# A gated attention block on one core: load order of the first tokens, shorter rotary angles, and the query latent between transposes

## The chip, the cores and the metric

The kernel runs on one core of a Trainium2 chip. The metric is the device time of one execution, in microseconds (us); the median of the runs before the change is 751.84. A core has five engines that run side by side: TensorE (PE in the profile; its weight loads are PEld), VectorE (DVE), ScalarE (ACT), GpSimd (POOL) and SyncE (SP), which here issues the transfers. A transfer is carried by 16 DMA engines, whichever engine issued it.

## The reference

One decoder layer on 512 tokens of width 1024, all in float32:

```
xn   = RMSNorm(x)
proj = xn @ w_in          # split into q_lat 384 | kv_lat 256 | k_rope 32 | dq, dk, dv 512 each | gates 2048
branch A: q = RMSNorm(q_lat) @ w_uq ; k, v = RMSNorm(kv_lat) @ w_ukv ; rotary on 32 dims ; causal attention, 8 heads
branch B: rotary on 16 of 64 dims ; (softmax(q1 k1) - lambda softmax(q2 k2)) v ; RMSNorm per head, 4 heads
merged = sigmoid(gate_a) * (o_a @ w_a) + sigmoid(gate_b) * (o_b @ w_b)
x = x + merged @ w_out
x = x + (silu(hn @ w_gate) * (hn @ w_up)) @ w_down,  hn = RMSNorm(x)
out = RMSNorm(x)
```

The rotary angles are position x inverse frequency; their sine and cosine are taken after the angle is reduced to a part of one turn.

## The kernel before, in words

**Products.** A float32 product is made from three products of a rounded type: each operand is split into `hi` (rounded) and `lo` (the residue, `src - hi`), and `mm3` (L299 to L303) adds hi x hi, hi x lo and lo x hi. Every weight and every activation that TensorE multiplies therefore needs two element-wise operations first: a rounding (a copy with a type change) and a residue (a subtraction). Which engine does which is set by lists: `W_DVE` names the latent weights whose rounding is on VectorE (the others are on ScalarE), `W_POOL` those whose residue is on GpSimd (the others on VectorE), and `W_ENG0`, `W_ENG`, `W_ENG_DIFF` do the same for the weights that `weights` loads later, in three stages.

**Tiles.** Tokens are in four tiles of 128 (`NB = 4`), the model width in eight chunks of 128 (`KD = 8`). `xts[t]` is token tile t as loaded, in two halves of 512 columns. `scaled_transpose(t0, t1)` transposes these tiles on TensorE (L347), scales with the norm's gain while it rounds out of PSUM (ACT, L353), and writes the residue (DVE, L355); the result is `xn`. The factor 1/rms is applied later, so that the products need not wait for it; `x_square` (L359) gathers the sums of squares.

**The first 50 us.** `LOADS` is the order of the first transfers, all issued by SP: `r` the gains and biases as rows (`rows`), `x0` to `x3` the token tiles, `A0` to `A6` two chunks each of the query-latent weights, `B0` to `B6` the same for the key-value latent, `i` the frequency column and the positions. `START` is the order of the work on them: `r` makes columns from `rows` by a transpose after eight dummy products (`columns`, L216), `t0`, `t1`, `t23` transpose token tiles, `d6` runs six dummy products, `a0`...`b7` split latent weights (`latent_weights`, L325), `s0`...`s3` are the sums of squares. Then come, in the order of the program, the norm factors, lambda (L387 to L393), the rotary angles (L398 to L417), their sines on ScalarE with a change of activation table before and after (L420 to L435), and the latents.

`latent(b)` (L443) multiplies token tiles by the latent weights: b = 0 the query latent (128 x 384, `PS("mm")`, and `"pv"` for the last tile), b = 1 key-value latent and rotary key (128 x 288). For each tile there are 8 chunks of 3 products; ACT then squares with a sum (L449) and copies (L451). After the first two tiles of b = 1 the rotary tables are multiplied out on TensorE (L540), then the rest follows, and then the fill work: gate products, projections and attention.

**Order.** A scheduler that simulates the engines orders each engine's instructions, by priority in the order of the program among what it takes to be ready. `tc.issue_after(x)` adds an order: instructions of the block on x's engine come behind x. Each engine works its instructions off in that order, so one that waits holds up all behind it. Slots of the pools (`L` 22, `w` 3, `raw` 4) come free when their users are done.

**The angles.** With `ahl` an angle in two parts, and a sum over five pieces of 1/(2 pi), a piece costs a multiply-and-round (L405, L406), a plain multiply (L407), a subtraction (L409 or L411) and, after the first, an addition (L412), all on VectorE on 128 x 256.

Of the kernel before, what the change touches and what calls it, by code (L numbers as in the profile page):

```python
# [16 lines left out]
AF = mybir.ActivationFunctionType  # L17
ALU = mybir.AluOpType
# [13 lines left out]
QR, KVR, RD = 384, 256, 32  # L32
# [4 lines left out]
MAGIC = 12582912.0  # L37
TWO_PI = 6.283185
BUFS = dict(X=2, L=22, P=6, PT=1, raw=4, w=3, t=5, sm=24)
LOADS = "r x0 A0 i A2 x1 A4 A6 x2 x3 B0 B2 B4 B6".split()  # L40
START = "r t0 d6 a0 a1 a2 a3 t1 s0 s1 a4 a5 a6 a7 t23 s2 s3 b0 b1 b2 b3 b4 b5 b6 b7".split()
TAB_T = 2
LAST = 256
W_POOL = "a0 a1 a4 b0 b1 b2 b3 b4 b5 b6 b7".split()
W_DVE = "b0 b1 b2 b3 b4 b5 b6 b7".split()
N_WARM = 8
P_POOL = (0, 1)
W_ENG0 = ['act', 'pool']
# [45 lines left out]
def build(ctx, nc, tc, a, out):  # L94
# [12 lines left out]
    def PS(tag):  # L107
        return pp.tile([P, 512], F32, name=nm("ps_" + tag), tag=tag, bufs=PBUFS[tag])
# [4 lines left out]
    def LF():  # L113
        return T("L", [P, 1024], F32)
# [4 lines left out]
    def sm(w=1):  # L119
        return T("sm", [P, w], F32)  # L120

    def r32(ap):
        return ap.bitcast(F32)

    def dma(o, i):
        nc.sync.dma_start(out=o, in_=i)
# [18 lines left out]


    LOG_EXP = "natural_log_exp_and_others"
    table = [nc.scalar.preload_act_table_set(LOG_EXP)]

    def load_log_exp(after):  # L150
        with tc.issue_after(after.ins):
# [18 lines left out]
    ones = sb.tile([P, P], F32, name="ones")  # L170
    nc.vector.memset(ones, 1.0)

    def load_x(t):
        for c in range(2):
            dma(xts[t][:, c * S:(c + 1) * S], a["x"][0, t * P:(t + 1) * P, c * S:(c + 1) * S])

    misc = T("PT", [P, 2560], F32)

    def latent_load(b, k):
        c0, n = ((0, QR), (C_KV, KVR + RD))[b]  # L180
        if b == 1 and k == 6:
            v = misc[:, 11 * P:11 * P + 2 * n]
        else:
            i = k % 4 if b == 0 else k
            v = r32(lat_raw[k // 4 if b == 0 else 2]).rearrange("p a b -> p (a b)")[:, i * n:(i + 2) * n]
        v = v.rearrange("p (a b) -> p a b", a=2)
        dma(v, kview("w_in", c0, n, k, 2))
        for j in range(2):
            lat_w[k + j][b] = v[:, j, :]

    lat_w = [[None, None] for _ in range(KD)]
    ccol = sb.tile([P, 2], F32, name="ccol")
    cst, lv = misc[:, 0:4 * P], misc[:, 4 * P:6 * P].rearrange("p (i d) -> p i d", i=4)
# [10 lines left out]
        dma(pos_i, a["positions"])  # L204

    for step in LOADS:
        k = int(step[1:] or 0)
        if step[0] == "x":
            load_x(k)
        elif step[0] == "r":  # L210
            dma(rows, a["rows"])
        elif step[0] == "i":
            small_inputs()
        else:
            latent_load("AB".index(step[0]), k)
    def columns():  # L216
        dummies(N_WARM)
        pc = PS("sc")
        nc.tensor.transpose(out=pc[:, :30], in_=rows, identity=ident[:30, :30])
        nc.vector.tensor_copy(out=cols, in_=pc[:, :30])  # L220
        nc.vector.tensor_scalar(out=cols[:, R_SG:R_SG + 1], in0=cols[:, R_SG:R_SG + 1], scalar1=1.0 - LAMBDA_INIT,
                                scalar2=None, op0=ALU.mult)
# [35 lines left out]
                                           op0=ALU.mult, op1=ALU.subtract)  # L258

    w_eng = list(W_ENG0)  # L260

    def round_hi(o, i):
        if w_eng[0] == 'act':
            nc.scalar.activation(out=o, in_=i, func=AF.Copy)  # L264
        else:
            nc.vector.tensor_copy(out=o, in_=i)

# [31 lines left out]
    def mm3(o, lhs, rhs, start, stop):  # L299
        (lh, ll), (rh, rl) = lhs, rhs  # L300
        nc.tensor.matmul(out=o, lhsT=lh, rhs=rh, start=start, stop=False)  # L301
        nc.tensor.matmul(out=o, lhsT=lh, rhs=rl, start=False, stop=False)  # L302
        return nc.tensor.matmul(out=o, lhsT=ll, rhs=rh, start=False, stop=stop)  # L303
# [16 lines left out]
        return [T("X", [P, 4, 2, S], F32R) for _ in range(2)]  # L320


    last_t, last_hi = [None], [None]

    def latent_weights(b, k):  # L325
        raw = lat_w[k][b]
        n = (QR, KVR + RD)[b]
        w = T("L", [P, 2, n], F32R)
        if "ab"[b] + str(k) in W_DVE:
            nc.vector.tensor_copy(out=w[:, 0, :], in_=raw)  # L330
        else:
            nc.scalar.activation(out=w[:, 0, :], in_=raw, func=AF.Copy)
        (nc.gpsimd if "ab"[b] + str(k) in W_POOL else nc.vector).tensor_sub(out=w[:, 1, :], in0=raw, in1=r32(w[:, 0, :]))
        lat_w[k][b] = [w[:, s, :] for s in range(2)]

# [3 lines left out]
    def scaled_transpose(t0, t1):  # L339

        n = t1 - t0
        for k0 in range(0, KD, 4 // n):
            pt = PS("tr" if k0 // (4 // n) % 2 == 0 else "sc")
            c = 0
            for k in range(k0, k0 + 4 // n):
                for t in range(t0, t1):
                    last_t[0] = nc.tensor.transpose(out=pt[:, c:c + P], in_=xts[t][:, k * P:(k + 1) * P], identity=ident)  # L347
                    c += P
            parts = [[pt[:, (k - k0) * n * P:(k - k0 + 1) * n * P]]
                     + [xn[k // 4][:, k % 4, s_, t0 * P:t1 * P] for s_ in range(2)] + [col(R_XG + k)]  # L350
                     for k in range(k0, k0 + 4 // n)]
            for src, hi, lo, g in parts:
                last_hi[0] = nc.scalar.activation(out=hi, in_=src, func=AF.Identity, scale=g)  # L353
            for src, hi, lo, g in parts:
                nc.vector.scalar_tensor_tensor(out=lo, in0=src, scalar=g, in1=r32(hi), op0=ALU.mult, op1=ALU.subtract)  # L355

    def x_square(t):
        with tc.issue_after(last_hi[0].ins):
            nc.scalar.activation(out=xts[t], in_=xts[t], func=AF.Square, accum_out=x_ss[:, t:t + 1])  # L359

    for step in START:
        k = int(step[1:2] or 0)
        if step[0] == "r":
            columns()
        elif step[0] == "d":
            with tc.issue_after(last_t[0].ins):
                dummies(int(step[1:]))
        elif step[0] in "ab":
            latent_weights("ab".index(step[0]), k)
        else:  # L370
            if step[0] == "s":
                x_square(k)
            else:
                scaled_transpose(k, int(step[-1]) + 1)

    dma(cst, a["cst"][:, 0:4 * P])
    dma(misc[:, 4 * P:6 * P], a["lambdas"].broadcast_to([P, 256]))

    def xa(k, sl=slice(None)):
        return [xn[k // 4][:, k % 4, s, sl] for s in range(2)]  # L380

    x_rs = rsqrt(x_ss, D, NB)
    x_ms = sm(NB)
    nc.vector.tensor_mul(out=x_ms, in0=x_rs, in1=x_rs)

    lp = lv[:, 0:4:2, :]
    nc.vector.tensor_mul(out=lp, in0=lv[:, 0:4:2, :], in1=lv[:, 1:4:2, :])  # L387
# [13 lines left out]
    ahl, acc, ry, rx = [v[:, c:c + 2 * P].rearrange("p (s n) -> p s n", s=2) for v in (tmp(), tmp()) for c in (0, 2 * P)]  # L401
    nc.vector.tensor_copy(out=ahl[:, 0, :], in_=r32(ah))
    nc.vector.tensor_sub(out=ahl[:, 1, :], in0=ang, in1=ahl[:, 0, :])
    for j, c in enumerate(_inv_2pi_pieces()):
        nc.vector.tensor_scalar(out=ry, in0=ahl, scalar1=c, scalar2=MAGIC, op0=ALU.mult, op1=ALU.add)  # L405
        nc.vector.tensor_scalar(out=ry, in0=ry, scalar1=MAGIC, scalar2=0.0, op0=ALU.subtract, op1=ALU.add)  # L406
        nc.vector.tensor_scalar(out=rx, in0=ahl, scalar1=c, scalar2=0.0, op0=ALU.mult, op1=ALU.add)  # L407
        if j == 0:
            nc.vector.tensor_sub(out=acc, in0=rx, in1=ry)  # L409
        else:  # L410
            nc.vector.tensor_sub(out=rx, in0=rx, in1=ry)  # L411
# [12 lines left out]
    for src in (turn_c, turn):  # L424
        tg = tmp()
        nc.gpsimd.memset(tg, 0.0)
        for q in range(4):
            with tc.issue_after(last_sin.ins):
                last_sin = nc.scalar.activation(out=tg[32 * q:32 * q + 32, q * P:(q + 1) * P],
                                                in_=src[32 * q:32 * q + 32, :], func=AF.Sin, scale=TWO_PI)  # L430
# [6 lines left out]
    latn = [LF() for _ in range(NB)]

    lat_ss = [sm(NB), sm(NB)]

    lat_mm = [None]

    def latent(b, t0=0, t1=NB):  # L443
        c0, n, ncol = ((0, QR, QR), (QR, KVR + RD, KVR))[b]
        for t in range(t0, t1):
            ps = PS("pv" if t == 3 and b == 0 else "mm")
            for k in range(KD):
                lat_mm[0] = mm3(ps[:, :n], xa(k, slice(t * P, (t + 1) * P)), lat_w[k][b], k == 0, k == KD - 1)
            nc.scalar.activation(out=latn[t][:, c0:c0 + ncol], in_=ps[:, :ncol], func=AF.Square,  # L449
                                 accum_out=lat_ss[b][:, t:t + 1])  # L450
            nc.scalar.activation(out=latn[t][:, c0:c0 + n], in_=ps[:, :n], func=AF.Copy)  # L451

    def latent_norm(b):
        c0, ncol = ((0, QR), (QR, KVR))[b]
# [68 lines left out]
    ps = PS("sc")  # L523
# [283 lines left out]
    for p in range(4):  # L807
        o = L_()
# [56 lines left out]
    x1 = []  # L865
# [135 lines left out]
```

## Time and profile before

| what | value |
|---|---|
| median of 3 runs | 751.84 us (751.84 to 752.97) |
| the profiled execution: time, span | 753.9 us, 752.1 us |
| mean granted TensorE clock | 0.993 |
| busy: PE, DVE, ACT, POOL | 737.0, 414.7, 326.8, 104.3 us |
| moved by DMA | 76.74 MB, mean 102 GB/s |

The span runs from the first to the last instruction; the profiled execution took 1.8 us more than its span, and 2.1 us more than the median. In the timeline a line has start, duration, engine, line of the kernel, operation, output and inputs, shape, count, and in brackets the idle time before it with what ended it. In the busy time by stages a line has the stretch, its length, busy time and count for PE, PEld, DVE, ACT and POOL, the granted clock, the share of the DMA engines and GB/s. In the waits a line has who waited for whom: total, times, longest.

### The profile page before, as it was taken

The numbers are of one execution on the slowest core, as the hardware profiler recorded it, in microseconds if no ns is written. First come the engines' busy times: TensorE is split into PE (matmuls) and PEld (weight loads), VectorE is DVE, ScalarE is ACT, GpSimd is POOL, SyncE is SP. The second block draws the span as 40 slices with busy tenths as digits, with TensorE's granted clock in tenths as the row PEclk, the third lists the DMA queues.
The fourth block names the chain that finished last, engine by engine and source line by source line (L and its number), as shares of the span: only waits on it lengthen the run. The fifth ranks groups of instructions, "written<-read, shape, count | busy, mean of one in ns | idle before, by whom it ended". The sixth has DMA issues, their size and how long they took to land.

```text
span 752.1 us, 9652 instructions
## 1 busy us (share of the span) xinstructions
PE 737.0 (98%) x3639; PEld 623.0 (83%) x3639; DVE 414.7 (55%) x800; ACT 326.8 (43%) x609; POOL 104.3 (14%) x94
## 2 busy tenths in 40 slices
PE   7999999999999999999999999999999999999996
PEld 5988889888888888788898888888888888888885
DVE  6968688898998745595453323333333332122424
ACT  6564558587667535644233323232322223122314
POOL 3505252631341001000000000000000000000302
PEclk9999999999999999999999999999999999999999
DMA  8404333552433322248023333333323232322203
GB/s 300 124 1 117 106 87 96 135 126 69 110 87 87 107 85 85 84 140 278 2 85 108 89 97 99 98 99 87 109 85 111 85 112 85 109 88 92 106 0 113
DMA packets 99820, 76.74 MB, mean 102 GB/s; under 512 B 6303, under 2 KB 86973, under 8 KB 99773
## 3 DMA queue, kind: packets, MB, share of 16 engines
q1 hardware_dynamic: 99773, 76.12, 34.3%
q8 instruction: 29, 0.48, 0.3%
q14 instruction: 18, 0.15, 0.1%
HBM read 69.81 MB, written 2.10 MB: 96 GB/s over the span
## 4 chain that ended last, share of the span: by engine, by line
PE 81%; DVE 9%; ACT 5%; POOL 2%; issue 2%; DMA 1%; SPq 0%; DVEq 0%; ACTq 0%
PE ps_mm L301 22%; PE ps_mm L303 22%; PE ps_mm L302 22%; PE ps_sc L633 2%; PE ps_sc L301 1%; PE ps_sc L302 1%; PE ps_tr L301 1%; PE ps_tr L302 1%; PE ps_tr L303 1%; PE ps_sc L303 1%; POOL t L567 1%; PE ps_tr L659 1%; ACT L L495 1%; DVE w L269 1%; DVE X L355 1%
## 5 line engine op out<-in xcount | busy, mean ns | idle before, releaser
L302 PE MATMUL ps_mm<-X,w 128*128 128x512 f32 (+1 forms) x568 | 217.0, 382 | 0.0
L301 PE MATMUL ps_mm<-X,w 128*128 128x512 f32 (+1 forms) x568 | 216.9, 382 | 0.1
L303 PE MATMUL ps_mm<-X,w 128*128 128x512 f32 (+1 forms) x568 | 216.6, 382 | 0.0
L269 DVE TENSOR_TENSOR w<-raw,w 128x1024 fp32r<-128x1024 f32 x92 | 116.3, 1266 | 165.4 <-ACT w L264 165.2
L264 ACT ACTIVATE w<-raw 128x1024 fp32r<-128x1024 f32 (+1 forms) x98 | 101.1, 1036 | 181.2 <-issue 78.9
L303 PEld LDWEIGHTS ps_mm<-X,w 128*128 128x128 f32 x568 | 106.9, 188 | 19.9 <-POOL w L269 0.3
L301 PEld LDWEIGHTS ps_mm<-X,w 128*128 128x128 f32 x568 | 106.7, 188 | 19.9 <-DVE t L565 0.2
L302 PEld LDWEIGHTS ps_mm<-X,w 128*128 128x128 f32 x568 | 106.8, 188 | 19.7 <-DVE X L255 0.2
L936 POOL TENSOR_TENSOR L<-L,P 128x512 f32<-128x512 f32 (+1 forms) x9 | 11.6, 1299 | 439.0 <-ACT t L935 439.0
L909 ACT ACTIVATE t<-ps_mm 128x512 f32<-128x512 f32 x22 | 13.2, 598 | 80.9 <-PE ps_mm L303 80.9
L910 DVE TENSOR_TENSOR t<-t,ps_mm 128x512 f32<-128x512 f32 x22 | 15.1, 688 | 59.7 <-PE ps_mm L303 59.7
L156 ACT ACTIVATE P<-P,sm 128x128 f32<-128x128 f32 (+3 forms) x64 | 35.8, 560 | 27.4 <-DVE sm L637 27.0
L269 POOL TENSOR_TENSOR w<-raw,w 128x1024 fp32r<-128x1024 f32 (+3 forms) x22 | 37.3, 1701 | 57.5 <-PE ps_tr L472 25.8
L633 PE MATMUL ps_sc<-L,L 96*128 96x128 f32 (+7 forms) x160 | 36.5, 327 | 1.5 <-DVE sm L637 1.5
L302 PE MATMUL ps_mm<-w,L 128*128 128x512 f32 (+1 forms) x100 | 37.2, 372 | 0.0
L301 PE MATMUL ps_mm<-w,L 128*128 128x512 f32 (+1 forms) x100 | 37.2, 374 | 0.0
L303 PE MATMUL ps_mm<-w,L 128*128 128x512 f32 (+1 forms) x100 | 37.1, 373 | 0.0
L301 PE MATMUL ps_mm<-L,w 128*128 128x512 f32 x90 | 35.2, 393 | 0.5 <-ACT w L264 0.5
L302 PE MATMUL ps_mm<-L,w 128*128 128x512 f32 x90 | 35.5, 394 | 0.0
L303 PE MATMUL ps_mm<-L,w 128*128 128x512 f32 x90 | 35.2, 393 | 0.0
L251 ACT ACTIVATE L<-t 64x512 fp32r<-64x512 f32 (+2 forms) x47 | 29.1, 623 | 13.6 <-POOL t L567 6.2
L255 DVE TENSOR_TENSOR L<-t,L 128x512 fp32r<-128x512 f32 (+2 forms) x37 | 29.6, 801 | 4.8 <-ACT L L251 4.5
(265 smaller groups left out, 1231.9 us busy)
## 6 DMA issues: line engine op xcount, KB each, us to landing
raw<-w_in SPq DMA_DIRECT2D x28, 512.0 KB, 4.0
raw<-w_ffn_gate SPq DMA_DIRECT2D x22, 512.0 KB, 3.9
raw<-w_ffn_up SPq DMA_DIRECT2D x22, 512.0 KB, 3.9
raw<-w_ffn_down SPq DMA_DIRECT2D x22, 512.0 KB, 3.6
L<-L SPq DMA_DIRECT2D x32, 128.0 KB, 2.9
raw<-w_out SPq DMA_DIRECT2D x8, 512.0 KB, 3.7
L<-x SPq DMA_DIRECT2D x8, 256.0 KB, 6.1
raw<-w_branch_mla SPq DMA_DIRECT2D x4, 512.0 KB, 3.4
```

What stands on the lines that cost most here:

```text
L156: return nc.scalar.activation(**kw)
L251: nc.scalar.activation(out=hi, in_=src, func=AF.Copy, scale=scale)
L255: nc.vector.tensor_sub(out=lo, in0=src, in1=r32(hi))
L264: nc.scalar.activation(out=o, in_=i, func=AF.Copy)
L269: (nc.vector if w_eng[1] == 'dve' else nc.gpsimd).tensor_sub(out=o, in0=i, in1=r32(hi))
L301: nc.tensor.matmul(out=o, lhsT=lh, rhs=rh, start=start, stop=False)
L302: nc.tensor.matmul(out=o, lhsT=lh, rhs=rl, start=False, stop=False)
L303: return nc.tensor.matmul(out=o, lhsT=ll, rhs=rh, start=False, stop=stop)
L633: nc.tensor.matmul(out=ps[:, :n], lhsT=q[:, i * P:n], rhs=k[:, 0:n], start=j == 0, stop=j == last)
L909: last_silu = nc.scalar.activation(out=g, in_=gate_ps, func=AF.Silu)
L910: nc.vector.tensor_mul(out=g, in0=g, in1=ps)
L936: nc.gpsimd.tensor_mul(out=xs, in0=xs, in1=g)
```

## The change

- Loads: the first token tile's halves come first; the frequency column and the positions, and then `rows`, are issued from ScalarE's queue (a `*` behind a step), ahead of its activation table load; halves of token tiles are now steps of their own.
- Order of the start: four dummies instead of six; `l002`, `l024`, `l048`, `l102` are pieces of the query latent (token tile, first and last chunk): tile 0 chunks 0 to 1, 2 to 3, 4 to 7, and tile 1 chunks 0 to 1. `latent` can now do a part of the chunks. Transposes that follow a piece are ordered behind it on TensorE; the sums of squares move behind the last transposes.
- Engines: no latent residue is on GpSimd any more (`W_POOL` empty), and the later weights of the first stage have their residue on VectorE; the roundings of `a0`, `a1`, `a4`, `a5` are on VectorE, those of `b0` to `b7` on ScalarE. New orders: latent weights from `a4` on behind the last rounding out of PSUM, the first stage's weight roundings behind the last latent weight's, the lambda product behind the last residue.
- Angles: a piece's plain multiply and subtraction become one `scalar_tensor_tensor`.

```diff
-LOADS = "r x0 A0 i A2 x1 A4 A6 x2 x3 B0 B2 B4 B6".split()
-START = "r t0 d6 a0 a1 a2 a3 t1 s0 s1 a4 a5 a6 a7 t23 s2 s3 b0 b1 b2 b3 b4 b5 b6 b7".split()
+LOADS = "x00 i* r* x01 A0 A2 x10 x11 A4 A6 x20 x21 x30 x31 B0 B2 B4 B6".split()
+START = "r t0 d4 a0 a1 a2 a3 l002 t1 l024 a4 a5 a6 a7 l048 l102 t23 s0 s1 b0 b1 b2 b3 s2 s3 b4 b5 b6 b7".split()
-W_POOL = "a0 a1 a4 b0 b1 b2 b3 b4 b5 b6 b7".split()
-W_DVE = "b0 b1 b2 b3 b4 b5 b6 b7".split()
+W_POOL = ()
+W_DVE = "a0 a1 a4 a5".split()
-W_ENG0 = ['act', 'pool']
+W_ENG0 = ['act', 'dve']
...
-    table = [nc.scalar.preload_act_table_set(LOG_EXP)]
+    table = [None]
...
     for step in LOADS:
+        issuer[0] = nc.scalar if step[-1] == "*" else nc.sync
...
+    issuer[0] = nc.sync
+    table[0] = nc.scalar.preload_act_table_set(LOG_EXP)
...
     def round_hi(o, i):
         if w_eng[0] == 'act':
-            nc.scalar.activation(out=o, in_=i, func=AF.Copy)
+            with tc.issue_after(last_w[0].ins):
+                nc.scalar.activation(out=o, in_=i, func=AF.Copy)
...
+    def latent(b, t0=0, t1=NB, k0=0, k1=KD):
+        c0, n, ncol = ((0, QR, QR), (QR, KVR + RD, KVR))[b]
+        for t in range(t0, t1):
+            if k0 == 0:
+                lat_ps[b, t] = PS("pv" if t == 3 and b == 0 else "mm")
+            ps = lat_ps[b, t]
+            for k in range(k0, k1):
+                lat_mm[0] = mm3(ps[:, :n], xa(k, slice(t * P, (t + 1) * P)), lat_w[k][b], k == 0, k == KD - 1)
+            if k1 < KD:
+                continue
...
         elif step[0] in "ab":
-            latent_weights("ab".index(step[0]), k)
-        else:
-            if step[0] == "s":
-                x_square(k)
+            if step[0] == "a" and k < 4:
+                latent_weights(0, k)
             else:
+                with tc.issue_after(last_hi[0].ins):
+                    latent_weights("ab".index(step[0]), k)
+        elif step[0] == "s":
+            x_square(k)
+        elif step[0] == "l":
+            latent(0, k, k + 1, int(step[2]), int(step[3]))
+        elif lat_mm[0] is not None:
+            with tc.issue_after(lat_mm[0].ins):
                 scaled_transpose(k, int(step[-1]) + 1)
+        else:
+            scaled_transpose(k, int(step[-1]) + 1)
...
     lp = lv[:, 0:4:2, :]
-    nc.vector.tensor_mul(out=lp, in0=lv[:, 0:4:2, :], in1=lv[:, 1:4:2, :])
+    with tc.issue_after(last_lo[0].ins):
+        nc.vector.tensor_mul(out=lp, in0=lv[:, 0:4:2, :], in1=lv[:, 1:4:2, :])
...
-        nc.vector.tensor_scalar(out=rx, in0=ahl, scalar1=c, scalar2=0.0, op0=ALU.mult, op1=ALU.add)
-        if j == 0:
-            nc.vector.tensor_sub(out=acc, in0=rx, in1=ry)
-        else:
-            nc.vector.tensor_sub(out=rx, in0=rx, in1=ry)
+        nc.vector.scalar_tensor_tensor(out=rx if j else acc, in0=ahl, scalar=c, in1=ry, op0=ALU.mult, op1=ALU.subtract)
+        if j > 0:
             nc.vector.tensor_add(out=acc, in0=acc, in1=rx)
...
-    latent(0)
+    latent(0, 1, 2, 2)
+    latent(0, 2)
     latent_norm(0)
```

More of the change, by code (lines that the diff above doesn't have):

```diff
@@ L123, in r32 @@
         return ap.bitcast(F32)
+    issuer = [nc.sync]
     def dma(o, i):
-        nc.sync.dma_start(out=o, in_=i)
+        issuer[0].dma_start(out=o, in_=i)
     tc.cur_priority = 1000000
@@ L171, in build, with load_x @@
     nc.vector.memset(ones, 1.0)
-    def load_x(t):
-        for c in range(2):
-            dma(xts[t][:, c * S:(c + 1) * S], a["x"][0, t * P:(t + 1) * P, c * S:(c + 1) * S])
+    def load_x(t, c):
+        dma(xts[t][:, c * S:(c + 1) * S], a["x"][0, t * P:(t + 1) * P, c * S:(c + 1) * S])
     misc = T("PT", [P, 2560], F32)
@@ L206, in build @@
     for step in LOADS:
+        issuer[0] = nc.scalar if step[-1] == "*" else nc.sync
+        step = step.rstrip("*")
         k = int(step[1:] or 0)
         if step[0] == "x":
-            load_x(k)
+            load_x(k // 10, k % 10)
         elif step[0] == "r":
@@ L260, in build @@
     w_eng = list(W_ENG0)
+    last_w = [None]
     def round_hi(o, i):
         if w_eng[0] == 'act':
-            nc.scalar.activation(out=o, in_=i, func=AF.Copy)
+            with tc.issue_after(last_w[0].ins):
+                nc.scalar.activation(out=o, in_=i, func=AF.Copy)
         else:
@@ L320, in norm_tiles @@
         return [T("X", [P, 4, 2, S], F32R) for _ in range(2)]
-    last_t, last_hi = [None], [None]
+    last_t, last_hi, last_lo = [None], [None], [None]
     def latent_weights(b, k):
@@ L331, in latent_weights @@
         else:
-            nc.scalar.activation(out=w[:, 0, :], in_=raw, func=AF.Copy)
+            last_w[0] = nc.scalar.activation(out=w[:, 0, :], in_=raw, func=AF.Copy)
         (nc.gpsimd if "ab"[b] + str(k) in W_POOL else nc.vector).tensor_sub(out=w[:, 1, :], in0=raw, in1=r32(w[:, 0, :]))
@@ L354, in scaled_transpose @@
             for src, hi, lo, g in parts:
-                nc.vector.scalar_tensor_tensor(out=lo, in0=src, scalar=g, in1=r32(hi), op0=ALU.mult, op1=ALU.subtract)
+                last_lo[0] = nc.vector.scalar_tensor_tensor(out=lo, in0=src, scalar=g, in1=r32(hi), op0=ALU.mult,
+                                                            op1=ALU.subtract)
     def x_square(t):
@@ L359, in x_square, with xa @@
             nc.scalar.activation(out=xts[t], in_=xts[t], func=AF.Square, accum_out=x_ss[:, t:t + 1])
+    def xa(k, sl=slice(None)):
+        return [xn[k // 4][:, k % 4, s, sl] for s in range(2)]
+    latn = []
+    lat_ss = [sm(NB), sm(NB)]
+    lat_mm = [None]
+    lat_ps = {}
+    def latent(b, t0=0, t1=NB, k0=0, k1=KD):
[8 more added lines that the diff above has]
+                continue
+            if b == 0:
+                latn.append(LF())
+            nc.scalar.activation(out=latn[t][:, c0:c0 + ncol], in_=ps[:, :ncol], func=AF.Square,
+                                 accum_out=lat_ss[b][:, t:t + 1])
+            nc.scalar.activation(out=latn[t][:, c0:c0 + n], in_=ps[:, :n], func=AF.Copy)
     for step in START:
@@ L368, in build @@
         elif step[0] in "ab":
-            latent_weights("ab".index(step[0]), k)
-        else:
-            if step[0] == "s":
-                x_square(k)
-            else:
-                scaled_transpose(k, int(step[-1]) + 1)
+            if step[0] == "a" and k < 4:
[10 more added lines that the diff above has]
+                scaled_transpose(k, int(step[-1]) + 1)
+        else:
+            scaled_transpose(k, int(step[-1]) + 1)
     dma(cst, a["cst"][:, 0:4 * P])
     dma(misc[:, 4 * P:6 * P], a["lambdas"].broadcast_to([P, 256]))
-    def xa(k, sl=slice(None)):
-        return [xn[k // 4][:, k % 4, s, sl] for s in range(2)]
     x_rs = rsqrt(x_ss, D, NB)
@@ L435, in build @@
     load_log_exp(last_sin)
[L437 to L451, printed above, removed]
     def latent_norm(b):
```

## The prediction

> **What bounds the kernel now.** First the page: which engine is full. Then the waits of the matmul engine (PE): where it is empty.
>
> ```profile
> span 752.1 us, 9652 instructions
> PE 737.0 (98%) x3639; PEld 623.0 (83%) x3639; DVE 414.7 (55%) x800; ACT 326.8 (43%) x609; POOL 104.3 (14%) x94
> ```
> ```profile
> PE ps_tr L347 <- DMA L<-x: 2.9, 1, 2.9
> PE ps_sc L633 <- DVE sm L637: 1.5, 1, 1.5
> PE ps_pv L169 <- DVE P L165: 1.2, 1, 1.2
> PE ps_mm L303 <- DVE X L355: 1.1, 1, 1.1
> PE ps_tr L540 <- DVE P L534: 0.6, 1, 0.6
> ```
>
> PE is busy 98% of the span, so only its idle time and its slow time can be won. The listed waits are 7.3 us, all but one (L633, at 78.8 us) in the first 45 us, where the change lies. The busy time by stages, with the granted clock (PEclk) behind POOL's column, shows the slow time:
>
> ```profile
> 4.84:11.23 6.39, 3.41 (x23) 2.22 (x23) 4.32 (x16) 4.36 (x14) 2.00 (x2) 1.00 1.00 336
> 11.23:15.16 3.93, 3.93 (x16) 3.93 (x15) 3.93 (x15) 3.93 (x12) 0.00 (x0) 0.57 1.06 396
> 15.16:29.40 14.24, 14.24 (x88) 13.82 (x87) 14.21 (x28) 8.41 (x19) 10.63 (x11) 1.00 0.57 163
> 29.40:30.64 1.24, 0.16 (x2) 0.00 (x1) 1.24 (x3) 0.00 (x0) 1.24 (x2) 1.00 0.39 64
> ...
> 77.30:83.00 5.70, 4.21 (x20) 3.88 (x20) 4.57 (x13) 2.65 (x8) 2.88 (x4) 0.71 0.86 233
> 83.00:740.00 657.00, 656.11 (x3197) 553.61 (x3197) 342.54 (x611) 274.27 (x479) 69.66 (x54) 1.00 0.33 95
> ```
>
> From 11.23 to 15.16 the first latent matmuls run at 0.57 of the clock; from 15.16 on VectorE (DVE) is busy 14.21 of 14.24 us, and PE then starves 1.08 us at 29.40. After 83 us PE idles 0.89 us in 657: nothing to win there. PE's timeline gives the marks:
>
> ```profile
> 5.77 1.46 PE L169 MATMUL ps_pv<-P 128*128 128x512 bf16 x6
> 10.11 0.66 PE L347 MATMUL ps_tr<-ident,L 128*128 128x128 f32 x4 [2.88 <-DMA L<-x]
> ...
> 11.25 0.55 PE L301 MATMUL ps_mm<-L,X 128*128 128x384 f32 x1
> ...
> 15.91 0.33 PE L302 MATMUL ps_mm<-L,X 128*128 128x384 f32 x1
> 16.08 0.33 PE L303 MATMUL ps_mm<-L,X 128*128 128x384 f32 x1
> ...
> 32.66 0.34 PE L303 MATMUL ps_pv<-L,X 128*128 128x384 f32 x1
> ...
> 43.39 1.20 PE L540 MATMUL ps_tr<-P,P 128*128 128x512 f32 x4 [0.61 <-DVE P L534]
> ```
>
> First latent matmul 11.25; last of the 96 of the query latent 32.66; the rotary tables (L540) 43.39. Starts lie 0.17 us apart at full clock.
>
> Why DVE is late shows in its own timeline beside POOL's:
>
> ```profile
> 7.12 0.23 DVE L398 CAST PT<-PT 128x128 f32<-128x128 int32 x1 [1.79 <-DMA PT<-positions]
> 8.22 1.12 DVE L403 TENSOR_TENSOR t<-PT,t 128x128 f32<-128x128 f32 x1
> 9.27 1.11 DVE L355 SCALAR_TENSOR_TENSOR X<-ps_tr,cols,X 128x128 fp32r<-128x128 f32 x4
> 10.31 0.28 DVE L405 TENSOR_SCALAR t<-t 128x256 f32<-128x256 f32 x1
> 10.51 0.28 DVE L407 TENSOR_SCALAR t<-t 128x256 f32<-128x256 f32 x1
> ...
> 11.94 1.02 DVE L333 TENSOR_TENSOR L<-w,L 128x384 fp32r<-128x384 f32 x2
> 12.88 0.42 DVE L409 TENSOR_TENSOR t<-t 128x256 f32<-128x256 f32 x1
> 17.07 0.52 DVE L330 CAST L<-w 128x288 fp32r<-128x288 f32 x2
> 26.60 2.44 DVE L387 TENSOR_TENSOR PT<-PT 128x128 f32<-128x128 f32 x1
> 28.96 1.23 DVE L411 TENSOR_TENSOR t<-t 128x256 f32<-128x256 f32 x1
> 30.11 0.87 DVE L355 SCALAR_TENSOR_TENSOR X<-ps_sc,cols,X 128x256 fp32r<-128x256 f32 x2
> ...
> 37.23 0.29 DVE L417 TENSOR_TENSOR PT<-PT,t 128x128 f32<-128x128 f32 x1
> ```
> ```profile
> 8.20 2.00 POOL L333 TENSOR_TENSOR L<-w,L 128x384 fp32r<-128x384 f32 x2 [5.23 <-ACT L L332]
> ...
> 26.49 4.28 POOL L269 TENSOR_TENSOR w<-raw,w 128x1024 fp32r<-128x1024 f32 x3
> ```
>
> L387 and L417 are the same operation on 128x128: 2.44 us just after POOL began a tensor_sub at 26.49, 0.29 with POOL idle. L403 (1.12) and L411 (1.23 against L409's 0.42) show the same beside POOL. Nine DVE operations between 8 and 30 us, L403 first and the L411 at 28.96 last, are longer in this way, by 7.6 us together. The 1.1 us stall of PE is the end of this: the residue of the last token tile (L355 at 30.11) stands behind L387 and L411.
>
> **The change part by part.**
>
> *The subtractions leave POOL.* W_POOL empty and W_ENG0 on DVE take 11 latent and 6 weight subtractions off POOL. DVE gains, at the pitch of starts: 3 residues 128x384 at 0.47 (L333, two in 0.94), 8 of 128x288 at about 0.37 (between 0.47 and the 0.34 of 128x256, which is L409's 0.42 less the 0.08 by which neighbours overlap, as L405's 0.28 ends in a next start after 0.20), 4 roundings 128x384 at about 0.27 (L330's two take 0.52): 1.4 + 3.0 + 1.1 = 5.5 us. Three weight residues (1024, 384, 256 wide) add 1.27 + 0.47 + 0.34 = 2.1, 1.27 being this row:
>
> ```profile
> L269 DVE TENSOR_TENSOR w<-raw,w 128x1024 fp32r<-128x1024 f32 x92 | 116.3, 1266 | 165.4 <-ACT w L264 165.2
> ```
>
> DVE loses the 7.6 us of blocking and eight roundings of 128x288 (0.22 each by L330's pitch, 1.8 us), which go to ScalarE (ACT); that engine idles 5.91 us here before its L156:
>
> ```profile
> 7.55 0.98 ACT L332 ACTIVATE L<-w 128x384 fp32r<-128x384 f32 x2
> ...
> 31.09 0.44 ACT L156 ACTIVATE sm<-sm 128x4 f32<-128x4 f32 x2 [5.91 <-DVE sm L236]
> ```
>
> Eight, each no longer than one of the wider L332's (0.49), are under 4 us and fit there; without that cover they cost those 4 us.
>
> *Rotary angles.* Five L407 go, and five subtractions become one fused operation each of the same shape: 5 x 0.20 = 1.0 us less (10.31 to 10.51). The fused form on SBUF operands is not in the trace; bounded by L409's 0.34 below and by 0.43 above (L355 at 30.11, two 128x256 in 0.87), the part is worth 0.5 to 1.0 us; I take 1.0. The lambda product L387 is ordered behind the last residue, which its cost can then no longer delay. DVE in sum: 7.6 - 7.6 - 1.8 - 1.0 = 2.8 us less, and it can begin the angles about 1.8 us earlier (the wait of L398).
>
> *Loads.* The three small inputs go to ACT's queue. On SP each took some 0.43 us of issue, as `positions` does in the SP timeline, 1.3 us for three, ahead of A0, A2 and the second token tile. The transfers, in 0.3 us bins from 0, show the hole they leave at 3.9 to 4.8 us (109, 94, 176):
>
> ```profile
> 3.12 0.43 SPq L126 DMA_DIRECT2D PT<-positions  x1
> ```
> ```profile
> GB/s 0 0 0 0 0 19 33 96 177 410 307 376 239 109 94 176 266 312 333 337 290 309 341 306 301 338 318 287 292 370 355 360 355 386 376 386 406 405 406 408
> ```
>
> Filling it to 320 GB/s moves later loads up by 0.6 us; at most the 1.3 us of issue, at least nothing. The activation table moves behind ACT's three issues: 1.4 us later, hidden, for ACT's first work comes at 5.5. The first half tile arriving earlier is worth nothing, since PE's opening dummies run to 4.74. The Trainium skill, "DMA: Bandwidth & Descriptors", "Issuing engines are not separate DMA queues", says that a second issuing engine saves only sequencer time; by it the part ends at that 1.3 us, and the hole in the transfers agrees. The danger is `rows`, now third on ACT: PE's column transpose stands in front of all others. Landing by 4.7 it costs nothing; at the 4.3 us that ccol took from issue to landing (below), issued near 1.7, it would land at 6.0 and cost 1.3. I take nothing.
>
> ```profile
> ccol<-cst SPq DMA_DIRECT2D x1, 1.0 KB, 4.3
> ```
>
> *Latents between the transposes.* On PE the second tile's transposes now wait for l002, the third and fourth's for l102; the squares and the b roundings wait on ACT for the last transposed tile's rounding, and weight roundings for the last latent weight's; behind them in ACT's order stands nothing that PE needs before the gate product, which comes after all latents. The first latent product needs the first tile's residues (DVE from 5.9: eight at 0.26, 2.1 us) and a0, a1 (four operations, 1.5 us): 8.0 if interleaved, 9.5 if not; I take 8.5, against 11.25. PE's work from there to the end of the query latent is 96 x 0.173 = 16.6 us plus 24 transposes at 0.11 (eight from 10.11 to about 11), 2.7: 27.8 at full clock. Two DVE-fed tiles give it 9.3 us of work until the later tiles land, so I expect little starving. PE again falls idle between four dummies (1.0 us, two fewer) and 8.5, so I charge the slow clock again: 11 matmuls in 3.93 us instead of 1.9, about 1.7 after rounding the mixed transposes: 29.5. Before it was 32.66 + 0.17 = 32.8. Gain 3.3 us; if start and starving go badly, 1.5; if all is fed and the clock full, 5.0.
>
> The clock is where the skill speaks against my charge. "TensorE: Matmul & The Clock Gate", "HAM oscillation", says that only idle gaps above about 3.4 us bring the half clock back. By that sentence the new gap of some 2 us would cost nothing and the sum would be 1.7 us better. This trace differs: 2.88 us idle before 10.11 was enough, and 1.47 us before 78.80 was followed by 0.71.
>
> *Rotary tables and beyond.* Before, tables came 5.9 us after the last angle (37.52 to 43.39). DVE ahead by between 2.8 and 4.6 us, tables would be ready at 38.8 to 40.6; PE arrives at 42.78 - 3.3 = 39.5. I let the 0.6 us stall vanish (a new stall of up to 1.1 us, so -0.5 to +0.6). Next late is DVE at 60 to 80 us, where it gets three more weight residues (1024, 512, 384 wide, 2.4 us) while losing blocking; the 1.47 us stall at L633 and the slow clock after it (1.4 us) I leave as they are, with ends of -2.0 and +2.9.
>
> **The sum.** 3.3 + 0.6 = 3.9 us off the profiled span of 752.1, thus 748.2. That run took 753.9; the median of the runs is 751.84, and the gain is taken from the median: 747.9.
>
> **The rivals.**
> 1. *More is won.* The clock stays full from the dummies on, or the stall at 78 us goes with POOL's load. For it: POOL leaves the start entirely. Against: two gaps shorter than 3 us brought the slow clock. 747.9 - 1.7 = 746.2 by the clock, which is the page's rule; 745.0 with the stall and its slow phase instead.
> 2. *Little is new.* Latents already run between transposes from 11.25 on, and loads are bound by bytes: the share of the DMA engines is 1.00 from 4.84. Then only the 1.1 us stall and the 0.6 of loads are won: 750.1, at the edge of no change.
> 3. *DVE becomes the bound (slower).* If the long operations are not POOL's doing, DVE carries 7.6 - 2.8 = 4.8 us more; angles end at 42.3 less the 1.8 of earlier start, tables come at 46.4. PE at 39.5 has all other work in order behind them: 6.9 us idle against 3.9 won, 754.8. It decides once tables come later than 43.4. L387's 2.44 against 0.29 speaks against it.
>
> **How the numbers follow.** The main case has 0.56 (746.3 to 749.7), more won 0.16 (the clock 0.09 of it), little new 0.20, DVE bound 0.08. About 0.2%, 1.5 us, separates a change from none: below 750.3 is faster. "Little new" lies on that edge, half on each side; of the main case 0.04 goes to no change as its tail. Faster 0.52 + 0.16 + 0.10 = 0.78, same 0.14, slower 0.08. The range from 745.0 to 751.2 leaves out the slow case and the far ends of the others.
>
> **What would show it.** Right: no POOL tensor_sub before 32 us and L387 under 0.4 us; first L301 into ps_mm near 8.5; end of the 384-wide matmuls near 29.5; no L303 wait on L355; L540 without a wait. Wrong: the column transpose later than 4.8 (rows), gaps of PE on L333 between 9 and 15, L540 waiting on P, a longer L633 wait near 75 us.

## The result and the profile after

| kernel | median of runs (us) | lowest to highest | ratio to before, 95% interval |
|---|---|---|---|
| before | 751.85 | 751.70 to 752.97 | 1 |
| after | 756.58 | 756.14 to 757.7 | 1.0063 [1.0051, 1.0076] |

The change makes the kernel 4.7 us slower. One slow run of the kernel before, 816.58 us, is left out of the range and the ratio. The profiled execution took 757.7 us, 1.1 more than the median; its span is 3.6 us above the span of before. First the head of the page after, then PE's waits, with the longest first.

```profile
span 755.7 us, 9635 instructions
PE 739.7 (98%) x3637; PEld 625.0 (83%) x3637; DVE 414.3 (55%) x808; ACT 325.6 (43%) x613; POOL 84.7 (11%) x77
```
```profile
PE ps_sc L658 <- DVE sm L662: 3.5, 1, 3.5
PE ps_mm L310 <- DVE L L341: 1.9, 1, 1.9
PE ps_mm L309 <- DVE L L338: 1.3, 1, 1.3
```

POOL has 20 us less work, DVE's total is what it was, and PE is busy 2.7 us longer with two products fewer: more of them run at the slow clock. Two waits of before are gone, as forecast: the product that waited for the last token tile's residue (1.1) and the rotary tables' (0.6; L540 is now L565). So is the longest, for a token tile (L347, 2.9). In their place stand 3.2 us ahead of the first products, and the scores' wait on the mask's maximum (L633 on L637 before, L658 on L662 now) grew from 1.5 to 3.5. PE's timeline shows where:

```profile
9.13 0.41 PE L309 MATMUL ps_mm<-L,X 128*128 128x384 f32 x1 [1.25 <-DVE L L338]
11.48 0.69 PE L310 MATMUL ps_mm<-L,X 128*128 128x384 f32 x1 [1.93 <-DVE L L341]
...
13.29 1.05 PE L355 MATMUL ps_tr<-ident,L 128*128 128x128 f32 x4
...
33.26 0.33 PE L311 MATMUL ps_pv<-L,X 128*128 128x384 f32 x1
...
43.88 1.09 PE L565 MATMUL ps_tr<-P,P 128*128 128x512 f32 x4
...
76.28 0.92 PE L658 MATMUL ps_sc<-L,L 96*128 96x128 f32 x6 [0.34 <-DMA L<-L]
77.04 0.28 PE L309 MATMUL ps_mm<-w,X 128*128 128x256 f32 x1
80.78 1.33 PE L658 MATMUL ps_sc<-L,L 96*128 96x384 f32 x3 [3.45 <-DVE sm L662]
81.90 0.41 PE L310 MATMUL ps_mm<-w,X 128*128 128x256 f32 x1
```

The first product comes 2.1 us earlier than before, but the second only at 11.48; the last of the query latent is at 33.26 (before 32.66), the tables at 43.88 (43.39). So the start won nothing, though little is lost by it up to 68.90 us either (first 128x256 product after the gates; before 68.64). From there on time is lost: the first score block is 1.3 us later than before (76.28, before 74.94), PE does one product (before: 13) between the second and the third score block, then waits 3.45 us (before: 1.47), and the products behind take 0.41 us instead of 0.28, at the slow clock.

VectorE's timeline, then GpSimd's, show who is late:

```profile
4.84 0.23 DVE L441 CAST PT<-PT 128x128 f32<-128x128 int32 x1 [3.31 <-DMA PT<-positions]
...
6.16 0.18 DVE L226 COPY cols<-ps_sc 128x30 f32<-128x30 f32 x1
...
7.60 1.12 DVE L363 SCALAR_TENSOR_TENSOR X<-ps_tr,cols,X 128x128 fp32r<-128x128 f32 x4
8.64 0.62 DVE L338 CAST L<-w 128x384 fp32r<-128x384 f32 x2
9.17 0.28 DVE L449 TENSOR_SCALAR t<-t 128x256 f32<-128x256 f32 x1
9.37 1.12 DVE L363 SCALAR_TENSOR_TENSOR X<-ps_sc,cols,X 128x128 fp32r<-128x128 f32 x4
10.41 1.01 DVE L341 TENSOR_TENSOR L<-w,L 128x384 fp32r<-128x384 f32 x2
...
61.26 1.23 DVE L277 TENSOR_TENSOR w<-raw,w 128x1024 fp32r<-128x1024 f32 x1
...
63.13 0.68 DVE L277 TENSOR_TENSOR w<-raw,w 128x512 fp32r<-128x512 f32 x1
...
74.16 0.67 DVE L274 CAST w<-raw 128x1024 fp32r<-128x1024 f32 x1
...
75.36 2.53 DVE L274 CAST w<-raw 128x1024 fp32r<-128x1024 f32 x1
...
78.41 2.10 DVE L274 CAST w<-raw 128x384 fp32r<-128x384 f32 x1
80.44 0.27 DVE L662 CUSTOM_DVE_ANT_0 P<-ps_sc,mask 128x128 f32<-128x128 f32 x1
```
```profile
74.96 2.38 POOL L277 TENSOR_TENSOR w<-raw,w 128x1024 fp32r<-128x1024 f32 x1 [1.88 <-ACT L L257]
77.96 2.34 POOL L277 TENSOR_TENSOR w<-raw,w 128x1024 fp32r<-128x1024 f32 x1 [0.63 <-DVE w L274]
```

The first mask maximum (L662) comes at 80.44, 2.0 us later than before (78.47). Two of the residues moved to VectorE stand at 61.26 and 63.13; behind them, two weight roundings (L274) take 2.53 and 2.10 us beside GpSimd's subtractions, where the same 128x1024 rounding took 0.67 at 74.16. These two were long before the change too (L266, 1.98 and 2.20 us), so what is new is mainly the work ahead of them. VectorE before, in the same stretch:

```profile
73.83 1.98 DVE L266 CAST w<-raw 128x1024 fp32r<-128x1024 f32 x1 [0.44 <-issue]
...
76.34 2.20 DVE L266 CAST w<-raw 128x384 fp32r<-128x384 f32 x1
78.47 0.27 DVE L637 CUSTOM_DVE_ANT_0 P<-ps_sc,mask 128x128 f32<-128x128 f32 x1
```

The busy time by stages, after and then before:

```profile
60.00:70.00 10.00, 10.00 (x52) 8.13 (x51) 9.81 (x17) 3.99 (x7) 1.10 (x1) 1.00 0.45 115
70.00:80.00 10.00, 6.92 (x39) 5.24 (x37) 9.97 (x12) 3.86 (x7) 5.40 (x3) 0.93 0.59 126
80.00:90.00 10.00, 9.22 (x56) 9.10 (x57) 5.15 (x18) 4.47 (x12) 2.17 (x4) 0.73 0.50 152
90.00:740.00 650.00, 649.38 (x3156) 547.36 (x3155) 338.08 (x599) 268.57 (x469) 68.02 (x53) 1.00 0.33 96
```
```profile
60.00:70.00 10.00, 10.00 (x52) 8.18 (x52) 9.06 (x17) 4.63 (x8) 5.22 (x3) 1.00 0.47 120
70.00:80.00 10.00, 8.51 (x53) 7.41 (x53) 9.47 (x14) 3.47 (x7) 6.88 (x4) 0.98 0.72 174
80.00:90.00 10.00, 10.00 (x71) 9.87 (x71) 4.43 (x19) 5.50 (x15) 1.71 (x4) 0.85 0.33 101
```

The third busy number is DVE's: 9.06 and 9.47 of 10 before, 9.81 and 9.97 after. PE loses 1.6 us in 70 to 80, 0.8 in 80 to 90, and runs there at 0.73 instead of 0.85. From 90 us on PE idles 0.6 us in 650: the loss lies before that.

### The profile page after: what moved, and what is told of

Same layout as the page of the kernel before. It is cut to its first block, busy times and chain, and to the rows that moved or that the text cites. A ratio compares the mean times of both kernels' runs of the same rounds, so it can differ in the third digit from the quotient of the medians.

```text
span 755.7 us, 9635 instructions
## 1 busy us (share of the span) xinstructions
PE 739.7 (98%) x3637; PEld 625.0 (83%) x3637; DVE 414.3 (55%) x808; ACT 325.6 (43%) x613; POOL 84.7 (11%) x77
## 4 chain that ended last, share of the span: by engine, by line
PE 84%; DVE 6%; ACT 5%; POOL 2%; issue 2%; DMA 1%; DVEq 0%; ACTq 0%; POOLq 0%
PE ps_mm L310 22%; PE ps_mm L311 22%; PE ps_mm L309 22%; PE ps_sc L658 2%; PE ps_sc L309 1%; PE ps_sc L310 1%; PE ps_tr L310 1%; PE ps_tr L309 1%; PE ps_tr L311 1%; PE ps_sc L311 1%; ACT L L519 1%; DVE L L261 1%; PE ps_tr L684 1%; ACT L L257 1%; ACT w L272 1%
## 5 line engine op out<-in xcount | busy, mean ns | idle before, releaser
L277 DVE TENSOR_TENSOR w<-raw,w 128x1024 fp32r<-128x1024 f32 (+1 forms) x98 | 120.5, 1232 | 167.3 <-ACT w L272 166.9
L658 PE MATMUL ps_sc<-L,L 96*128 96x128 f32 (+7 forms) x160 | 38.6, 332 | 3.8 <-DVE sm L662 3.5
L277 POOL TENSOR_TENSOR w<-raw,w 128x1024 fp32r<-128x1024 f32 (+3 forms) x16 | 28.7, 1794 | 93.6 <-DVE w L274 75.7
L662 DVE CUSTOM_DVE_ANT_0 P<-ps_sc,mask 128x128 f32<-128x128 f32 (+3 forms) x64 | 30.6, 478 | 5.7 <-PE ps_sc L658 5.6
```

What stands on the lines that cost most here:

```text
L277: (nc.vector if w_eng[1] == 'dve' else nc.gpsimd).tensor_sub(out=o, in0=i, in1=r32(hi))
L658: nc.tensor.matmul(out=ps[:, :n], lhsT=q[:, i * P:n], rhs=k[:, 0:n], start=j == 0, stop=j == last)
L662: nc.vector.tensor_tensor_reduce(out=m, in0=ps[:, :n], in1=mask[:, S - n:], scale=-1.0, scalar=3.4e38, op0=ALU.add, op1=ALU.min, accum_out ...
```

## The experiments

Theory A: the loss is made at 70 to 86 us; the weight residues that `W_ENG0` put on VectorE make it late for the first scores, and PE's planned order (third score block ahead of twelve value products instead of behind them) makes the wait longer. Theory B: the loss is the start (rows late, VectorE's order, transposes behind the latents' pieces, slow clock). Times are medians, ratios are against the kernel before.

**1. The six weight residues back on GpSimd** (label e1), and the same single edit in the kernel before, the other way round (e4):

```diff
-W_ENG0 = ['act', 'dve']
+W_ENG0 = ['act', 'pool']
```

> The changed kernel with the residues of the later first-stage weights back on GpSimd (W_ENG0 alone undone). Theory A (the loss lies at 70 to 86 us: these residues make VectorE late for the first scores, and the planned order puts the third block of scores ahead of twelve products that ran in that wait before): the wait at the scores falls from 3.5 to about 1.5 us, the slow clock after it shortens, time about 753.2. Theory B (the loss is the start: late gains rows, late first latent products): unchanged, about 756.5.

> The kernel before with W_ENG0's residues on VectorE, nothing else of the change. Theory A: slower by about 3 us, 754.9, with a wait of 3 us or more at the third block of scores. Theory B: no change or a shade faster, 751 to 752, since GpSimd no longer blocks VectorE at 26 to 31 us.

e1: 752.71 us, 1.0008 [0.9999, 1.0017]; the score wait is 1.5 us again. e4: 755.46 us, 1.0049 [1.0036, 1.0061]. PE's first wait in e4, and its stages:

```profile
PE ps_sc L633 <- DVE sm L637: 3.7, 1, 3.7
```
```profile
60.00:70.00 10.00, 10.00 (x56) 8.28 (x55) 9.87 (x18) 3.30 (x7) 1.10 (x1) 1.00 0.53 126
70.00:80.00 10.00, 6.16 (x29) 4.65 (x28) 9.94 (x13) 3.36 (x7) 6.69 (x4) 0.85 0.66 162
```

One list entry, alone, makes the old kernel 3.6 us slower, with the same full VectorE and the same wait; taken back, it gives the new one 3.9. Theory A holds for the residues; what PE's order adds is weighed in experiment 3.

**2. Only the three late residues back on GpSimd** (e8), the three early ones (at 33 to 35 us) staying on VectorE:

```diff
+    w_eng[:] = ['act', 'pool']
     fill(FILL[2])
```

> The changed kernel, with its three early weight residues on VectorE as changed, and the three late ones (1024, 512 and 384 wide, at 56 to 64 us) on GpSimd again. Theory A (the loss is VectorE late for the first scores, through those three late residues): the wait of the scores on the mask's maximum falls from 3.5 us to about 1.5, as it did when all six were on GpSimd; time 752.5 to 753. Rival (the early three on a VectorE that is full from 15 to 30 us push all that follows): the wait stays above 3 us and the time is 755 to 757.

751.93 us, 1.0001 [0.9992, 1.0010]; score wait 1.5 us. 4.65 us come back (756.58 to 751.93), the whole loss: the three early residues cost nothing that can be measured.

**3. The score block's place in PE's order.** The third score block held behind 12 (e5) or 24 (e6) value products in the changed kernel, and behind 24 in the kernel before (b6):

```diff
-                    mm3(ps[:, t * 256:(t + 1) * 256], ...)
+                    m = mm3(ps[:, t * 256:(t + 1) * 256], ...)
+                    if (c, tp, t, k) == (0, 0, 0, 3):    # (0, 1, 0, 3) for 24
+                        held.append(m)
...
+                if held and i == 2:
+                    with tc.issue_after(held[0].ins):
+                        nc.tensor.matmul(out=ps[:, :n], lhsT=q[:, i * P:n], rhs=k[:, 0:n], ...)
```

> The changed kernel with one edit in the order of the matmuls: the third block of scores of the first head is placed behind the first twelve products of the differential values, where the order of before had it; residues stay on VectorE. Theory A1 (most of the loss is the order: twelve ready products stand behind a score that waits): the wait shrinks by 12 x 0.12 = 1.4 us to about 2.0 us and the slow clock after it by a few matmuls; time 754 to 755. Theory A2 (VectorE is late by itself, and PE only waits later): no change, 756.5.

> As the one with twelve, behind 24 products. Theory A1: the wait shrinks by 2.9 us to about 0.6 us, the clock stays full, time 751.5 to 752.5. Theory A2: 756.5.

> The kernel before with the same one edit (third block of scores behind 24 products of the values). Theory A1: its wait of 1.47 us and the slow clock after it (1.4 us) go, time 749. Theory A2: 751.8.

e5: 755.37 us, 1.0042 [1.0030, 1.0055]; e6: 756.25, 1.0055 [1.0041, 1.0069]; b6: 755.22, 1.0046 [1.0033, 1.0058]. The scores' wait in e5, the longest wait in e6, and that in b6:

```profile
PE ps_sc L663 <- DVE sm L671: 1.8, 1, 1.8
```
```profile
PE ps_mm L309 <- DVE L L263: 2.5, 1, 2.5
```
```profile
PE ps_mm L301 <- DVE L L257: 3.4, 2, 2.3
```

Order is worth about 1.2 of the 4.7 us (the intervals of e5 and of the changed kernel overlap a little). Held further back, the score block no longer waits long, but a value product ahead of it waits for VectorE's residue instead, so that e6 gains nothing clear of noise where 4 to 5 us were expected. In b6, where a gain was expected, the kernel before became 3.4 us slower; only part of this lies at the scores, for from 90 us on PE idles 1.8 us more than before, 1.1 of it at 142.01, again behind a residue of VectorE. In the two orders tried, PE could not be given other work: VectorE itself was late for what came next.

**4. Pieces of the start.** Rows first again (e2), no latent pieces between the transposes (e3), twelve dummies instead of four (e7):

```diff
-LOADS = "x00 i* r* x01 A0 A2 ...
+LOADS = "r x00 i* x01 A0 A2 ...                                        # e2
-START = "r t0 d4 a0 a1 a2 a3 l002 t1 l024 a4 a5 a6 a7 l048 l102 t23 ...
+START = "r t0 d4 a0 a1 a2 a3 t1 a4 a5 a6 a7 t23 ...                    # e3
+START = "r t0 d12 a0 a1 a2 a3 l002 t1 l024 a4 a5 a6 a7 l048 l102 t23   # e7
```

> The changed kernel with the gains' rows issued first, from SyncE, as before the change. Theory A: the columns are ready near 4.9 instead of 6.2 us, the last 384-wide latent product ends some 1 us earlier, but VectorE stays as late at the scores relative to the matmuls; time 755.6. Theory B: start is all, 753 or less. A third view, that the wait at 77 us is set by VectorE's own chain from the start on: 756.5, since what PE gains it waits.

> The changed kernel without the pieces of the query latent between the transposes (the latent in one call behind them; all else as changed). Theory A: the second tile's transposes run near 10 us instead of 13.3, so the slow-clock stretch of the first products ends near 15 instead of 17 us; last 384-wide product about 1.5 us earlier, time 755.2, the wait at the scores stays. Theory B: 752 to 753.

> The changed kernel with twelve instead of four dummy products behind the first tile's transposes, which fill PE's idle time up to the first latent products. If the slow clock at 11 to 17 us comes from that idle time, the products run at full clock from 11.5 on and the last 384-wide product ends some 2 us earlier (31.3); the score's wait, set by VectorE, then grows, and the time falls by 0.5 to 2 us: 754.5 to 756. If the clock is set by something else (transposes not counting as work): no change.

e2: 757.45 us, 1.0078 [1.0065, 1.0090], no gain. The column transpose came at 4.72 instead of 5.57, but the copy of the columns stood behind four rotary operations on VectorE and came at 6.12 instead of 6.16. Late rows cost nothing in this order of VectorE. e3: 758.22, 1.0085 [1.0071, 1.0099]: PE finished the query latent 2.1 us earlier (31.14), only to wait for ScalarE's evacuation (L396) of the tiles that now end close together:

```profile
PE ps_mm L309 <- ACT L L396: 2.7, 1, 2.7
```

So the pieces are worth about 1.6 us (the intervals overlap), where a gain from leaving them out was expected. e7: 755.77, 1.0049 [1.0036, 1.0062], some 0.8 us better than four dummies, less than the intervals can separate; the wait of the first product falls from 1.3 to 0.5, that of the second stays at 1.9. The query latent's end, expected at 31.3 with a full clock, comes at 32.09; the clock from 11 to 18 us is 0.76, as it is in e5, e6 and e9 with four dummies, so the dummies are not shown to have raised it.

**5. The first two latent weights as before** (e10), on e1's kernel: rounded on ScalarE, residues on GpSimd.

```diff
-W_POOL = ()
-W_DVE = "a0 a1 a4 a5".split()
+W_POOL = "a0 a1".split()
+W_DVE = "a4 a5".split()
```

> The changed kernel with the six residues on GpSimd, and the first two latent weights split as before the change: rounded on ScalarE, residues on GpSimd. Theory B (VectorE's queue, with rotary operations ahead of these two, is what makes the second product come at 11.48 instead of 9.2): the wait of L310 on L341 (1.9 us) goes, and the time falls by 1 to 1.9 us against the kernel with the six residues alone moved (752.7): 750.8 to 751.7. Rival (what is won at the start is idle time that comes back, by the later tiles' transposes and by GpSimd blocking VectorE): 752.5 to 754.

752.31 us, 1.0002 [0.9993, 1.0010], 0.4 below e1 and so nearer the rival than theory B. PE's timeline:

```profile
9.04 0.44 PE L309 MATMUL ps_mm<-L,X 128*128 128x384 f32 x1 [1.08 <-ACT L L340]
10.12 0.44 PE L310 MATMUL ps_mm<-L,X 128*128 128x384 f32 x1 [0.64 <-POOL L L341]
...
31.09 0.33 PE L311 MATMUL ps_pv<-L,X 128*128 128x384 f32 x1
```

The second product comes 1.4 us earlier and the query latent ends 2.2 us earlier than in the changed kernel: these two residues in VectorE's queue were what spoilt the start. Yet little of it reaches the end while the scores' 1.5 us wait stands.

**6. The stage of the scores cleared.** The weight roundings of the first attention stage on ScalarE, in the changed kernel with e1's edit (e9), in the kernel before (b9), and with both e1's and the fifth experiment's edits (e11):

```diff
-        w_eng[:] = W_ENG
+        w_eng[:] = ['act', 'pool'] if p == 0 else W_ENG
```

> The changed kernel with the six residues on GpSimd, and the roundings of the weights of the first attention stage (among them L274 1024, 1024 and 384 wide between 72 and 79 us, on VectorE and lengthened to 2.0 and 2.2 us beside GpSimd's residues) on ScalarE, which is busy 3.5 of 10 us there. Theory A (VectorE's queue ahead of the first mask maximum sets that stage): the score wait of 1.5 us goes and the slow clock stays away; time 750.5 to 751.5, below the kernel before. Rival (ScalarE's queue ahead of its evacuations becomes the late one, or the roundings only move the wait to the next user): 752 to 754.

> The kernel before the change, with nothing altered but the roundings of the first attention stage's weights, on ScalarE instead of VectorE. If VectorE's queue ahead of the first mask maximum sets that stage in this kernel too, its score wait of 1.5 us and the slow clock behind it go: 751.8 less 1.5 to 2.9, so 749 to 750.3; and then the start of the changed kernel adds nothing, since the changed kernel with the same edits took 750.5. Rival (the start of the change is what gained, and the edit helps only behind it): 751.5 to 752.

> The changed kernel with the six residues on GpSimd, the roundings of the first attention stage on ScalarE (alone 750.5) and the first two latent weights split on ScalarE and GpSimd (alone 752.3, where the trace led by 1.7 us up to the scores and lost it in a slow clock behind the score wait). If a lead of the start is kept once nothing waits at the scores: 748.3 to 749.2. Rival (it is given back by the engine that is full anyway): 750 to 751.

| kernel | start | median (us) | ratio [interval] |
|---|---|---|---|
| b9 | before | 750.51 | 0.9976 [0.9967, 0.9985] |
| e9 | changed | 750.50 | 0.9978 [0.9969, 0.9987] |
| e11 | changed, first two weights as before | 749.48 | 0.9957 [0.9944, 0.9971] |

Busy time by stages of e9, and of b9:

```profile
70.00:80.00 10.00, 10.00 (x67) 9.00 (x66) 5.78 (x17) 6.95 (x16) 6.55 (x5) 1.00 0.85 197
80.00:90.00 10.00, 10.00 (x83) 9.80 (x81) 5.27 (x20) 7.08 (x18) 0.94 (x3) 1.00 0.21 72
```
```profile
70.00:80.00 10.00, 9.26 (x62) 8.25 (x61) 6.12 (x16) 6.75 (x14) 6.54 (x5) 1.00 0.78 187
80.00:90.00 10.00, 10.00 (x81) 9.70 (x80) 5.17 (x19) 6.94 (x18) 0.85 (x2) 1.00 0.25 85
```

DVE falls from 9.5 of 10 us to about 6, ScalarE rises to 7, the scores' wait on the mask's maximum is gone in both (b9 keeps 0.7 us there, for a transfer), and the clock stays at 1.00. The old and the new start, with that stage cleared, give the same time: the changed start has no value of its own. With its first two weights put back (e11) it has 1.0 us, between what the two theories gave, the intervals just touching. e11 is the fastest of all, 2.4 us below the kernel before and 7.1 below the changed one.

## Why the prediction was wrong

The forecast was 3.9 us faster, the result 4.7 slower, 8.6 apart. The runs divide it: 4.65 by the three late residues (experiment 2), and the forecast 3.9 of the start, which came to nothing (e8 and before are equal, and so are e9 and b9).

- **"The 1.47 us stall at L633 ... I leave as they are, with ends of -2.0 and +2.9": the step that failed most.** The text counted the three residues (2.4 us) into a VectorE that is 9.06 and 9.47 of 10 us busy there, and took the lost blocking as a counterweight. Here it was little: the two roundings that GpSimd holds up just ahead of the first scores stand beside the attention stage's own subtractions, which the change leaves on GpSimd (4.18 us together before, 4.63 after). The term measured 4.65 us, beyond its own end of +2.9: the mask maximum 2.0 us later, the changed order of PE (about 1.2 of the whole), and the slow clock behind a wait of 3.45. A longer L633 wait was named among the signs of a wrong prediction. The main case put it at nothing, and the range, up to 751.2, had room for the +2.9 (750.8) but not for 4.65 (752.6).
- **First product at 8.5, query latent's end at 29.5: failed.** The step was VectorE's order. The forecast let it begin the first token tile's residues at 5.9 us and do only these eight and four operations on a0 and a1, which end at 9.5 at the latest. But four rotary operations went ahead of them, they began at 7.60, and the residues of a0 and a1 ended at 11.42. The first product, which waits only for a rounding, came at 9.13; the second, which waits for the residue, at 11.48, 2.8 us later than 8.5 + 0.17. From there to 33.43 PE took 21.95 us for 95 products and 24 transposes, 19.1 at full clock by the forecast's own pitch; so the slow clock cost some 2.9 instead of the 1.7 charged. The 2.8 and this 1.2 make up the 3.9 by which the end was missed.
- **VectorE's 5.5 us more of work against 7.6 less of blocking: right in sum, wrong in place.** Up to 60 us VectorE was busy 42.30 us instead of 44.86, 2.6 less where 2.8 was forecast. No tensor_sub of GpSimd stands before 66 us, the lambda product takes 0.28 us, and the last angle ends at 29.3 us instead of 37.5. But what PE waited for at the start was not the angles, it was a0's residue, which GpSimd had made before, beside VectorE. The change took work from an idle engine and put it, in the first 12 us, into the queue that decided.
- **Rotary angles: right.** The fused operation is recorded with 0.41 to 0.43 us, as the subtraction alone was (0.42), so the part is worth the 1.0 us taken; no path of PE ran over it.
- **Loads.** Positions landed at 4.84 instead of 7.12 us; rows were late (transpose at 5.57) and this cost nothing (e2), as taken, though for a reason not given: VectorE's order, not the landing, sets the columns.
- **L540's stall gone: right, by luck.** There is no wait at L565, but because PE came there at 43.88, not at 39.5. The tables were forecast to be ready at 38.8 to 40.6; the last of their operands (L559 on VectorE) was done at 42.96, only 0.4 earlier than before (43.33). The step that failed is "behind them in ACT's order stands nothing that PE needs before the gate product": the sines stand there. The angles were done at 29.3, 8.2 us earlier than before, but ScalarE, with sums of squares and roundings in front, took them at 33.90, and loaded its table for the sines 2.0 us earlier than before (the last line):

```profile
33.90 0.30 ACT L460 ACTIVATE t<-PT 128x128 f32<-128x128 f32 x1
...
35.94 1.28 ACT L469 ACT_TABLE_LOAD   x1
```
```profile
37.89 1.28 ACT L429 ACT_TABLE_LOAD   x1
```

  In e10, whose query latent ends 2.2 us earlier, this operand is done at 41.68 and PE comes at 41.73. So this chain leaves PE no room to come earlier still; that was not tested by an edit.
- **Rivals 1 and 2.** More is won: the clock did not stay full (0.56 from 11 to 18 us, behind idle times of 1.25 and 1.93 us), and the stall at the scores grew. Little is new: for the start alone it came nearest, since e8, with the new start and without the late residues, is at 751.93, where it forecast 750.1.
- **Rival 3** named the right engine and the right sign at the wrong place: the tables, not the scores. Its premise, that GpSimd does not cause the long operations, is refuted (0.28 us for the lambda product), and its sign, tables later than 43.4, was met barely (43.88) and without a wait, so it does not explain the loss.

What stays open: that the new start's earlier angles, gone stalls and latent pieces add up to nothing was shown only as a sum. The trace says where the angles' lead went (ScalarE, above); by edits only the first two weights (1.0 us) and the pieces (1.6) were taken apart. The second tile's transposes, behind `l002` at 13.29 instead of 10.11, were not tried apart from the pieces. Of the 2.3 us by which e10's query latent ends earlier than e1's (31.09, 33.43), 1.7 are still there at the third score block (77.44, 79.15) and 0.2 at the fourth (82.19, 82.43): the products between them ran at the slow clock in e10's profile (0.80 from 74 to 82 us) and at the full one in e1's.

## What to carry to other kernels

An engine's load is to be counted stage by stage, for the stages that a list entry also reaches: 2.4 us onto a VectorE that was 93% busy ahead of the first scores cost 4.65. "POOL blocks VectorE" is a reason to move work only if the work then lands in a queue with room; here the room was on ScalarE, and moving one stage's roundings there gained 1.3 us in the kernel before and 2.2 in e1. And a wait that changes its partner when PE's order is changed (e6, b6) says that the engine behind it is the bound: these orders moved the wait and did not mend it.

## What the runs showed of the hardware

A VectorE rounding with a single input, 128x1024, took 2.53 us beside a GpSimd subtraction and 0.67 without; it ended at 77.89, 0.55 after GpSimd's operation, so it did next to nothing until that was over. The prediction's rows had shown this for operations on two tensors. The Trainium skill, "SBUF — State Buffer", "SBUF: two separate sides", says that the port pair that the two engines share is locked for a whole instruction and not split; the trace agrees.

The clock after an idle time is not the same from one execution to the next. The kernel before and b9 have the same start, and from 11 to 18 us (before, then b9):

```profile
11.00:18.00 7.00, 7.00 (x37) 6.91 (x37) 6.97 (x23) 5.75 (x17) 1.56 (x2) 0.76 1.07 385
```
```profile
11.00:18.00 7.00, 7.00 (x47) 6.62 (x46) 6.97 (x23) 7.00 (x20) 1.88 (x3) 1.00 1.08 391
```

0.76 and 1.00, and the tables come at 43.39 and 43.08: where VectorE is full (6.97 of 7), a faster clock is worth 0.3 us. With the changed start the same stretch had 0.53 to 0.58 in the profiles of the changed kernel, e1 and e8, and 0.76 in those of e5, e6 and e9. Likewise the scores' wait of 1.5 us was followed by 0.91 (72 to 90 us) in the kernel before and in e10, and by 1.00 in e1 and e8. The Trainium skill, "TensorE: Matmul & The Clock Gate", "Part 1: The HAM clock gate", says that the window that watches the activity runs freely, so that the number of slow products varies between runs; these pairs agree. A charge for the slow clock is then a range, not a number.
